# Forget gates' running sums: the triangle made on chip, and their store and first loads back issued by ScalarE

## The chip, the cores and the metric

The kernel runs on one core of a Trainium2 chip. The core has five engines, each with its own queue of instructions worked off in order: TensorE (PE; its weight loads are PEld), VectorE (DVE), ScalarE (ACT), GpSimd (POOL) and SyncE (SP), which here only issues DMAs. Engines wait for each other and for DMAs by semaphores. The metric is the device time of one execution in microseconds, lower being better; several runs are given by their median.

## The reference

A trunk of two layers over 1040 tokens (16 learned meta tokens and 1024 inputs) of width 1024. Each layer normalises, projects with one combined matrix, runs four heads of differential attention and eight heads of forgetting attention, gates both with SiLU, projects back and adds to the residual. Only the forgetting heads use the sums that the change touches:

```python
fq = ...; fk = ...; fv = ...                       # (b, 8 heads, tokens, 64)
log_f = jax.nn.log_sigmoid(ff.astype(jnp.float32) + forget_bias[l])
cum_logf = jnp.transpose(jnp.cumsum(log_f, axis=1), (0, 2, 1))   # (b, 8, tokens)
...
s = jnp.einsum('bhqd,bhkd->bhqk', qb, k) * scale   # forgetting_attention
s = s + cq[..., None] - cum_logf[:, :, None, :]
s = jnp.where(positions[None, :] <= pq[:, None], s, -jnp.inf)
p = jax.nn.softmax(s, axis=-1)
```

## The kernel before, in words

Tokens lie in nine blocks (80 tokens, seven of 128, 64), three blocks to a chunk, and the work on a layer is woven from two streams. The first is attention: 8 pairs of heads p, of which p = 0 to 3 are differential and p = 4 to 7 forgetting, each over three chunks. The second, the fills, are the projections: units k, q, v and g (gate) for each pair, in the order of the table ORDER. The order on TensorE is written out by the program (it is followed as emitted); on the other engines a scheduler sets the order, and SyncE's DMAs stand in an order of their own.

Weights come as 128x2x128 pieces by SyncE (line 254, tile wst, four buffers), are split into two parts (whi by ScalarE or GpSimd, lines 261 and 263; wlo by GpSimd or VectorE, line 265; eight buffers each), and feed TensorE's matmuls into pj (line 181, the line of every matmul).

The unit v2 (the values of the first forgetting heads) also projects the forget gates, eight columns, into ffz (z in the code). When its last block is done, log_forget computes the log-sigmoid by a chain of small VectorE operations on 128x72 (lines 544 to 561, with one exponential on ScalarE, line 546); line 561 writes the result to ffz. Some time later, by the program's model of TensorE's time, cumulate is emitted: it needs the upper triangle of ones (tile upper, which has the name tc, three buffers), multiplies each block's ffz with it (sums within a block, nine products into three sc tiles in PSUM, 4 passes in float32), and line 577 on VectorE adds the last sum of the block before while it writes the row crow (8 heads x 1040, a cb tile; two buffers). Line 579 stores crow to DRAM (cscr). When the first chunk of a forgetting pair begins, line 823 loads two rows of cscr back, each broadcast over 128 partitions, into cb tiles; line 656 on VectorE adds them to the scores of that head.

Around cumulate stand, in ScalarE's order, lines 778 and 780 (two copies of po, the attention output that TensorE has just finished, into ta), line 664 (the exponential of the last differential scores, tile e), and line 428 (q's two parts from pj). VectorE's line 716 then combines the two exponentials of a differential pair in e, which TensorE turns (tp, line 185). Line 804 makes TensorE's column sums of ta (sc<-ones,ta).

A constant of two 128x128 tables in bfloat16 (cb16: identb, the identity, and trib, 1e30 above the diagonal and 0 elsewhere) is loaded once at the start, for other uses.

Of the kernel before, what the change touches and what calls it, by code (L numbers as in the profile page):

```python
# [13 lines left out]
ALU = mybir.AluOpType  # L14

P = 128
# [4 lines left out]
T = N_META + SEQ  # L21
# [46 lines left out]
C_ID, C_U, C_DM, C_DM0 = 0, 128, 256, 256 + T  # L68
# [18 lines left out]
def trunk_kernel(ctx, tc, x, meta, norm_gain, w_in, fbias, lq1, lk1, lq2, lk2,  # L87
                 subln, w_out, fgain, cst, cstb, rope, out):
    nc = tc.nc
# [7 lines left out]
    dma = nc.sync.dma_start  # L97
# [4 lines left out]
    identb, trib = cb16[:, 0:P], cb16[:, P:2 * P]  # L102
# [25 lines left out]
    def st(tag, w, dt=F32, bufs=None):  # L128
        bufs = bufs or {"tc": TCB}.get(tag, 3)
        return sb.tile([P, w], dt, name=tag, tag=tag, bufs=bufs)  # L130

    def big(tag, bufs, dt=F32):
        return sb.tile([P, T], dt, name=tag, tag=tag, bufs=bufs)
# [25 lines left out]
    cscr = dr.tile([depth, 8, T], F32, name="cscr")  # L159
# [19 lines left out]
    def mm(o, a, b, start, stop, passes=1):  # L179
        n = b.shape[-1]  # L180
        nc.tensor.matmul(o, a, b, start=start, stop=stop)  # L181
        pe.add(b.dtype == BF16, max(n * passes * COL, 0.056))
# [29 lines left out]
    def proj_ps(tag="pj"):  # L212
        return ps.tile([P, 512], F32, name=tag, tag=tag, bufs={"pj": 2, "sc": SB, "tp": TB}[tag])
# [326 lines left out]
    def log_forget(l, z, box):  # L540

        n = NB * 8
        az = st("tc", CW)[:, :n]
        nc.vector.scalar_tensor_tensor(az, z, -1.0, z, ALU.mult, ALU.max)
        e = st("tc", CW)[:, :n]
        nc.scalar.activation(e, az, AF.Exp, scale=-1.0)

        d = st("tc", CW)[:, :n]
        nc.vector.tensor_scalar(d, e, 2.0, None, ALU.add)
        nc.vector.reciprocal(d, d)  # L550
        s = az
        nc.vector.tensor_tensor(s, e, d, ALU.mult)
        w = d
        nc.vector.tensor_tensor(w, s, s, ALU.mult)
        q = e
        nc.vector.tensor_scalar(q, w, 1.0 / 15, None, ALU.mult)
        for i in (13, 11, 9, 7, 5, 3):
            nc.vector.scalar_tensor_tensor(q, q, 1.0 / i, w, ALU.add, ALU.mult)
        nc.vector.scalar_tensor_tensor(q, q, 1.0, s, ALU.add, ALU.mult)
        nc.vector.tensor_scalar(z, z, 0.0, None, ALU.min)  # L560
        nc.vector.scalar_tensor_tensor(z, q, -2.0, z, ALU.mult, ALU.add)

        def cumulate():
            crow = big("cb", 2)
            upper = st("tc", CW)
            dma(out=upper[:, 0:P], in_=cst[:, C_U:C_U + P])
            for c in range(3):
                pt = proj_ps("sc")
                for j in range(3 * c, 3 * c + 3):
                    sz = BE[j] - BS[j]  # L570
                    o = BS[j] - CS[c]
                    mm(pt[:8, o:o + sz], z[:sz, j * 8:(j + 1) * 8], upper[:sz, :sz], True, True, 4)
                for j in range(3 * c, 3 * c + 3):
                    o = BS[j] - CS[c]
                    sz = BE[j] - BS[j]
                    prev = crow[:8, BS[j] - 1:BS[j]] if j else zero1[:8, :]
                    nc.vector.tensor_scalar(crow[:8, BS[j]:BE[j]], pt[:8, o:o + sz], prev, None,
                                            ALU.add)
            dma(out=cscr[l], in_=crow[:8, :])
            box["cum"] = True  # L580
            when["cum"] = pe.t + LCUM
        return cumulate
# [226 lines left out]
    def attention(l, box):  # L809


        units = [Unit(l, p, s, c, box) for p in range(8) for c in range(3)
                 for s in range(1 if p < 4 else 2)]

        def score(u, step):
            if not u.begun:
                u.begun = True
                if u.c == 0 and u.s == 0:
                    box["sp"] = u.p
                    for s in range(0 if u.diff else 2):  # L820
                        cb = box["cb", s] = big("cb", 2)
                        h = 2 * (u.p - 4) + s
                        dma(out=cb, in_=cscr[l, h:h + 1, :].to_broadcast([P, T]))
            u.score(*step)

        def there(u):

            return all(x in box and when.get(x, 0.0) <= pe.t + SLACK
                       for x in (("k", u.p, u.c), ("q", u.p, u.c), "cum")[:2 if u.diff else 3])

        late = []
        todo = units[0].score_steps()
        yield 0.0, ("k", 0, 0)
        yield 0.0, ("q", 0, 0)
        while todo:
            yield pe.evicted[0], None
            score(units[0], todo.pop(0))
        for i, u in enumerate(units):
            nx = units[i + 1] if i + 1 < len(units) else None
            todo = nx.score_steps() if nx else []  # L840
            free = EB - 3
            if nx and nx.diff:
                free = 2 * free - 1
            if nx and nx.p != u.p and not nx.diff:
                free = 0
            n = u.nblk
            seq = [("t", j) for j in range(TB)]
            for j in range(n):
                seq.append(("a", j))
                if j + TB < n:  # L850
                    seq.append(("t", j + TB))
            nt = due = 0
            yield u.ready, ("v", u.p, 0)
            box["vp"] = u.p
            for k, (what, j) in enumerate(seq):
                if late and pe.t >= late[0][0]:
                    late.pop(0)[1]()
                    yield 0.0, None
                if what == "t":
                    u.transp(j)  # L860
                    nt += 1
                else:
                    yield u.ev[j][2], ("v", u.p, j)
                    u.av(j)
                yield 0.0, None
                due += nt >= FR0 and k % FR1 == FR1 - 1
                if todo and (nt == n or (free > 0 and due > 0)) and there(nx):
                    free -= 1
                    due -= 1
                    yield pe.evicted[0], None  # L870
                    score(nx, todo.pop(0))
                    yield 0.0, None
            for t0, f in late:
                yield t0, None
                f()
            late = u.finish()
            while todo:
                yield 0.0, ("k", nx.p, nx.c)
                if not nx.diff:
                    yield 0.0, "cum"  # L880
                yield pe.evicted[0], ("q", nx.p, nx.c)
                score(nx, todo.pop(0))
                yield 0.0, None
        for t0, f in late:
            yield t0, None
            f()
# [327 lines left out]
```

## Time and profile before

| | us |
|---|---|
| median of 3 runs | 1623.01 |
| lowest, highest of them | 1619.45, 1624.98 |
| the profiled execution's own time | 1622.79 |
| its span (first to last instruction) | 1620.9 |

| engine | busy us | share of the span |
|---|---|---|
| PE | 1486.1 | 92% |
| PEld | 1419.7 | 88% |
| DVE | 1056.3 | 65% |
| ACT | 829.6 | 51% |
| POOL | 688.5 | 42% |

How to read the profile: it is one execution taken by the hardware profiler, in microseconds from the span's start. An operation is named by line, engine, operation and "out<-in". Where an engine stood idle ahead of an instruction, the idle time and what ended it stand in brackets ("[16.30 <-DMA tc<-in_cst_dram]"); a wait for several things is put down to the one that came last. The chain of waits follows the work back from the last instruction. A table of stretches gives each engine's busy time in a stretch and the clock granted to TensorE (1.00 is 2.4 GHz, 0.50 is 1.2 GHz).

### The profile page before, as it was taken

What the parts mean: (1) busy time and instruction counts of PE and PEld (TensorE: products, weight loads), DVE (VectorE), ACT (ScalarE), POOL (GpSimd) and SP (SyncE); (2) the same over time, 40 slices, a digit from 0 to 9 for tenths busy, and PEclk for the clock granted to TensorE, in tenths of its full rate; (3) what the DMA queues carried; (4) which work ended last, traced back from release to release, by engine and by line L of the source; (5) the groups of instructions that cost most, each with busy time, mean ns of one, the idle gap of its engine ahead of it and who ended that gap; (6) DMA issues with size and microseconds to landing.
All of it is one profiled execution on the core that took longest, in us unless ns stands there. A gap on an engine that the chain in (4) does not pass through costs nothing.

```text
span 1620.9 us, 30144 instructions
## 1 busy us (share of the span) xinstructions
PE 1486.1 (92%) x9932; PEld 1419.7 (88%) x9932; DVE 1056.3 (65%) x3024; ACT 829.6 (51%) x2067; POOL 688.5 (42%) x1125
## 2 busy tenths in 40 slices
PE   6988999978999999987998999999599999996897
PEld 5988999977999999887988898999599999995897
DVE  6588867864756565666655986596556555657554
ACT  6455556533655565543334655565256555655543
POOL 3453423312444344456756243240244442443664
PEclk9999999998999999988999999999799999998999
DMA  9342313202232323464434242131222232334554
GB/s 240 86 100 60 97 46 63 60 19 71 69 68 63 103 58 99 151 184 133 146 78 104 62 96 73 33 75 28 64 58 67 58 93 57 92 114 143 151 148 137
DMA packets 181469, 147.86 MB, mean 91 GB/s; under 512 B 19624, under 2 KB 176864, under 8 KB 181312
## 3 DMA queue, kind: packets, MB, share of 16 engines
q1 hardware_dynamic: 181312, 145.93, 33.9%
q8 instruction: 79, 1.29, 0.3%
q14 instruction: 78, 0.64, 0.1%
HBM read 117.49 MB, written 28.38 MB: 90 GB/s over the span
## 4 chain that ended last, share of the span: by engine, by line
PE 57%; DVE 11%; DMA 8%; issue 6%; POOL 3%; ACT 2%; SPq 0%; DVEq 0%; POOLq 0%; ACTq 0%
PE pj L181 36%; PE sc L181 8%; PE po L181 7%; PE tp L185 6%; DMA wst<-in_w_out_dram 3%; DMA wst<-in_w_in_dram 2%; DVE wlo L265 2%; POOL wlo L265 1%; DVE e L656 1%; DMA oscr<-ta 1%; DMA actl<-oscr 1%; DVE actl L430 1%; DVE atl L748 1%; DMA tc<-in_cst_dram 1%; DVE kt L430 1%
## 5 line engine op out<-in xcount | busy, mean ns | idle before, releaser
L181 PE MATMUL pj<-acth,whi 128*128 128x320 f32 (+2 forms) x1536 | 519.5, 338 | 15.8 <-DVE hc L942 9.9
L181 PE MATMUL pj<-acth,wlo 128*128 128x320 f32 (+2 forms) x1536 | 498.6, 325 | 0.0
L181 PE MATMUL pj<-actl,whi 128*128 128x320 f32 (+2 forms) x1536 | 498.4, 324 | 0.0
L265 POOL TENSOR_TENSOR wlo<-wst,whi 128x256 fp32r<-128x256 f32 (+1 forms) x320 | 251.6, 795 | 185.4 <-ACT whi L261 140.1
L181 PEld LDWEIGHTS pj<-acth,whi 128*128 128x128 f32 x1536 | 296.9, 193 | 19.4 <-DVE hc L942 6.6
L181 PEld LDWEIGHTS pj<-acth,wlo 128*128 128x128 f32 x1536 | 296.0, 193 | 0.5
L181 PEld LDWEIGHTS pj<-actl,whi 128*128 128x128 f32 x1536 | 294.6, 192 | 0.4 <-DVE actl L430 0.4
L664 ACT ACTIVATE e<-e,mn 80x80 f32<-80x80 f32 (+8 forms) x288 | 225.7, 784 | 123.5 <-DVE mn L656 121.0
L748 DVE TENSOR_TENSOR atl<-tp,ath 128x320 fp32r<-128x320 f32 (+8 forms) x432 | 191.6, 449 | 81.8 <-ACT ath L747 77.6
L747 ACT ACTIVATE ath<-tp 128x320 fp32r<-128x320 f32 (+8 forms) x432 | 168.3, 404 | 128.3 <-PE tp L185 119.1
L261 ACT ACTIVATE whi<-wst 128x256 fp32r<-128x256 f32 (+1 forms) x304 | 124.6, 415 | 139.7 <-PE pj L181 53.0
L181 PE MATMUL sc<-kt,qq 128*128 128x296 f32 (+9 forms) x480 | 175.6, 368 | 15.8 <-DVE mn L656 11.5
L185 PE MATMUL tp<-ident,e 128*128 128x128 f32 (+2 forms) x1080 | 179.8, 274 | 0.7 <-POOL e L697 0.3
L697 POOL TENSOR_SCALAR e<-e,rl 80x80 f32<-80x80 f32 (+2 forms) x144 | 109.0, 758 | 161.6 <-DVE rl L696 151.1
L181 PE MATMUL po<-ath,v 128*128 128x256 f32 (+5 forms) x576 | 164.9, 327 | 10.1 <-ACT ath L747 10.1
L181 PE MATMUL pj<-whi,acth 128*128 128x256 f32 (+3 forms) x576 | 166.6, 289 | 4.1 <-DVE v L430 3.3
L181 PE MATMUL pj<-wlo,acth 128*128 128x256 f32 (+3 forms) x576 | 163.6, 284 | 2.8 <-POOL wlo L265 1.4
L181 PE MATMUL pj<-whi,actl 128*128 128x256 f32 (+3 forms) x576 | 163.1, 283 | 0.8 <-POOL actl L406 0.8
L181 PE MATMUL sc<-kt,ql 128*128 128x296 f32 (+9 forms) x480 | 158.2, 332 | 0.0
L181 PE MATMUL po<-atl,v 128*128 128x256 f32 (+5 forms) x432 | 137.3, 318 | 18.2 <-DVE atl L748 17.9
L185 PEld LDWEIGHTS tp<-ident,e 128*128 128x128 f32 (+2 forms) x1080 | 136.5, 139 | 6.5 <-POOL e L697 1.9
L265 DVE TENSOR_TENSOR wlo<-wst,whi 128x256 fp32r<-128x256 f32 (+1 forms) x128 | 88.5, 696 | 62.4 <-POOL whi L263 53.0
(166 smaller groups left out, 2483.5 us busy)
## 6 DMA issues: line engine op xcount, KB each, us to landing
wst<-in_w_in_dram SPq DMA_DIRECT2D x256, 128.0 KB
wst<-in_w_out_dram SPq DMA_DIRECT2D x192, 128.0 KB
cb<-cscr SPq DMA_DIRECT2D x16, 520.0 KB
cb<-in_rope_dram SPq DMA_DIRECT2D x20, 320.0 KB
cb<-in_rope_dram SPq DMA_DIRECT2D x16, 384.0 KB
oscr<-ta SPq DMA_DIRECT2D x26, 160.0 KB
cb<-in_rope_dram SPq DMA_DIRECT2D x12, 336.0 KB
oscr<-ta SPq DMA_DIRECT2D x20, 192.0 KB
```

The source lines that it names most:

```text
L181: nc.tensor.matmul(o, a, b, start=start, stop=stop)
L185: nc.tensor.transpose(o, a, idn)
L261: nc.scalar.activation(hi, sg_, AF.Copy)
L265: eng.tensor_tensor(lo, sg_, hi.bitcast(F32), ALU.subtract)
L430: nc.vector.tensor_tensor(lo, src, hi.bitcast(F32), ALU.subtract)
L656: nc.vector.tensor_tensor_reduce(e[rows, a:b], pt[rows, :b - a], bias(a, b)[rows, :], op0=ALU.add, op1=ALU.min, scale=1.0, scalar=least, a ...
L664: nc.scalar.activation(e[rows, :ext], e[rows, :ext], AF.Exp, scale=-1.0, bias=mn[rows, len(pcs) - 1:len(pcs)], accum_out=l[rows, :])
L697: nc.gpsimd.tensor_scalar(e[rows, :ext], e[rows, :ext], r[rows, 0:1], 1.0, ALU.mult, ALU.mult)
L747: nc.scalar.activation(ah[:kz, n0:w], tp[:kz, n0:w], AF.Copy)
L748: nc.vector.tensor_tensor(al[:kz, n0:w], tp[:kz, n0:w], ah[:kz, n0:w].bitcast(F32), ALU.subtract)
```

## The change

The triangle is no longer loaded from DRAM: VectorE computes min(trib, 1) + identity into the same tile from the two bfloat16 tables. The store of crow and the two loads back for p = 4, the first forgetting pair, are issued by ScalarE; the loads back for p = 5 to 7 stay with SyncE.

```diff
@@ -563,7 +563,7 @@
         def cumulate():
             crow = big("cb", 2)
             upper = st("tc", CW)
-            dma(out=upper[:, 0:P], in_=cst[:, C_U:C_U + P])
+            nc.vector.scalar_tensor_tensor(upper[:, 0:P], trib, 1.0, identb, ALU.min, ALU.add)
...
-            dma(out=cscr[l], in_=crow[:8, :])
+            nc.scalar.dma_start(out=cscr[l], in_=crow[:8, :])
...
-                        dma(out=cb, in_=cscr[l, h:h + 1, :].to_broadcast([P, T]))
+                        load = nc.scalar.dma_start if u.p == 4 else dma
+                        load(out=cb, in_=cscr[l, h:h + 1, :].to_broadcast([P, T]))
```

The changed kernel has one line more, so line 823 is 824 there. TensorE's and GpSimd's orders are unchanged. On ScalarE, at the place of the sums in layer 0 (tc is the logarithm's tile, ta the two copies of po, e the differential scores, qq a part of q):

```order
 L261 ACTIVATE whi<-wst 128x256
 L546 ACTIVATE tc<-tc 128x72
+L579 DMA cscr<-cb 8x1040
 L778 ACTIVATE ta<-po,sgs_82 128x384
 L780 ACTIVATE ta<-po 128x384
-L664 ACTIVATE e,ls<-e,mn 128x976
+L824 DMA cb<-cscr 128x1040
+L664 ACTIVATE e,ls<-e,mn 128x976
+L824 DMA cb<-cscr 128x1040
 L428 ACTIVATE qq<-pj 64x336 x2
```

The store now stands on ScalarE ahead of the two copies, and the two loads stand around the exponential; the same holds in layer 1.

On SyncE, the same place in layer 0 (line 601 loads and line 790 stores attention outputs, line 254 loads weights):

```order
 L790 DMA oscr<-ta 128x336
 L254 DMA wst<-in_w_in_dram 128x2x128 x8
-L566 DMA tc<-in_cst_dram 128x128
-L579 DMA cscr<-cb 8x1040
-L601 DMA ta<-oscr 128x336
-L823 DMA cb<-cscr 128x1040
-L790 DMA oscr<-ta 128x384
-L823 DMA cb<-cscr 128x1040
+L601 DMA ta<-oscr 128x336
+L790 DMA oscr<-ta 128x384
 L254 DMA wst<-in_w_in_dram 128x2x128 x4
```

Four issues leave SyncE's order, and the two that stood among them close up.

On VectorE, the place in layer 1 (tc<-cb_67 is the triangle made from the tables; lines 660 and 656 evict scores):

```order
 L558 SCALAR_TENSOR_TENSOR tc<-tc 128x72 x6
 L559 SCALAR_TENSOR_TENSOR tc<-tc 128x72
+L566 SCALAR_TENSOR_TENSOR tc<-cb_67 128x128
 L561 SCALAR_TENSOR_TENSOR ffz<-tc,ffz 128x72
 L577 TENSOR_SCALAR cb<-sc,zero_79 8x80
 L577 TENSOR_SCALAR cb<-sc,cb 8x128 x7
+L577 TENSOR_SCALAR cb<-sc,cb 8x64
 L660 TENSOR_SCALAR e,mn<-sc 128x488
-L577 TENSOR_SCALAR cb<-sc,cb 8x64
 L656 ISA e,mn<-sc,dm,mn 128x488
```

The new operation stands between lines 559 and 561, and the last of the sums has moved ahead of the eviction of line 660; in layer 0 only the new operation is added, at the same place.

## Rows read from the trace of the kernel before

**Rows 1.** The page's first line: span of the profiled execution.
```profile
span 1620.9 us, 30144 instructions
```

**Rows 2.** TensorE's waits, longest first: us in total, times, longest us.
```profile
PE sc L181 <- DMA tc<-in_cst_dram: 33.8, 2, 17.5
PE po L181 <- DVE atl L748: 17.9, 17, 3.1
```

**Rows 3.** Chain that ended last, both layers: start us, us, what.
```profile
365.98 5.37 DMA tc<-in_cst_dram
...
1157.03 6.25 DMA tc<-in_cst_dram
```

**Rows 4.** Timeline, layer 0: start us, us, instruction [idle before <-releaser].
```profile
365.98 0.23 DVE L559 SCALAR_TENSOR_TENSOR tc<-tc 128x72 f32<-128x72 f32 x1
366.25 0.23 DVE L561 SCALAR_TENSOR_TENSOR ffz<-tc,ffz 128x72 f32<-128x72 f32 x1
371.48 3.43 PE L181 MATMUL sc<-tc,ffz 80*8 80x80 f32 x18 [16.30 <-DMA tc<-in_cst_dram]
```

**Rows 5.** Timeline, layer 1, the same place.
```profile
1157.30 0.23 DVE L561 SCALAR_TENSOR_TENSOR ffz<-tc,ffz 128x72 f32<-128x72 f32 x1
...
1163.41 3.41 PE L181 MATMUL sc<-tc,ffz 80*8 80x80 f32 x18 [17.53 <-DMA tc<-in_cst_dram]
```

**Rows 6.** Busy us (instructions) by stretch: length, PE, PEld, DVE, ACT, POOL, PEclk, DMA share, GB/s.
```profile
376.50:480.00 103.50, 103.50 (x709) 100.19 (x708) 59.86 (x194) 57.20 (x143) 46.31 (x86) 1.00 0.30 75
1168.40:1275.00 106.60, 106.17 (x725) 101.62 (x725) 62.30 (x199) 57.85 (x146) 47.08 (x96) 1.00 0.28 73
1158.00:1163.30 5.30, 0.00 (x0) 0.00 (x0) 0.00 (x0) 0.00 (x0) 0.00 (x0) 0.50 0.58 84
366.00:370.00 4.00, 0.00 (x0) 0.00 (x0) 0.45 (x2) 0.00 (x0) 0.00 (x0) 0.50 0.36 57
358.00:359.00 1.00, 0.00 (x0) 0.00 (x0) 0.17 (x1) 0.80 (x2) 0.51 (x1) 0.50 0.64 131
375.00:376.00 1.00, 1.00 (x7) 0.91 (x8) 0.93 (x5) 0.00 (x0) 0.00 (x0) 1.00 0.00 0
```

**Rows 7.** VectorE's groups by form, 340 to 380 us: busy us, mean ns.
```profile
L432 DVE SCALAR_TENSOR_TENSOR v<-pj,v 128x128 fp32r<-128x128 f32 x6 | 1.7, 287 | 1.5 <-ACT v L428 1.5
...
L552 DVE TENSOR_TENSOR tc<-tc 128x72 f32<-128x72 f32 x1 | 0.7, 723 | 0.0
```

**Rows 8.** Timeline: a matmul that TensorE starts on VectorE's signal.
```profile
703.70 0.48 DVE L748 TENSOR_TENSOR atl<-tp,ath 80x320 fp32r<-80x320 f32 x1
...
704.23 0.41 PE L181 MATMUL po<-atl,v 80*128 80x320 f32 x1 [1.02 <-DVE atl L748]
```

**Rows 9.** Timeline, layer 0, behind the restart: SyncE, ScalarE, VectorE, TensorE.
```profile
376.25 0.34 SPq L579 DMA_DIRECT2D cscr<-cb  x1
...
377.22 0.48 ACT L780 ACTIVATE ta<-po 128x384 f32<-128x384 f32 x1
...
377.71 1.11 ACT L664 ACTIVATE e<-e,mn 128x976 f32<-128x976 f32 x1
378.06 0.32 SPq L823 DMA_DIRECT2D cb<-cscr  x1
...
379.41 1.24 DVE L716 SCALAR_TENSOR_TENSOR e<-e,rl 128x976 f32<-128x976 f32 x1
380.43 0.45 ACT L428 ACTIVATE qq<-pj 64x336 fp32r<-64x336 f32 x1 [1.51 <-PE pj L181]
...
383.97 0.83 PE L185 MATMUL tp<-ident,e 128*80 128x128 f32 x6
```

**Rows 10.** Timeline, layer 1: the last sum on VectorE, and TensorE's tp.
```profile
1168.44 0.27 DVE L577 TENSOR_SCALAR cb<-sc,cb 8x64 f32<-8x64 f32 x1
...
1176.77 0.83 PE L185 MATMUL tp<-ident,e 128*80 128x128 f32 x6
```

**Rows 11.** VectorE's evictions that use the loaded sums: ns min/median/max, first and last start.
```profile
L656 DVE CUSTOM_DVE_ANT_0 e<-sc,cb x144: 222/521/668, 397.5 to 1481.0; 80x80 f32<-80x80 f32 x16, 128x208 f32<-128x208 f32 x16, 128x336 f32<-128x336 f32 x16, 128x464 f32<-128x464 f32 x16
```

## The prediction, made before the changed kernel was run

> **What bounds the kernel now.** I read the page first: the profiled execution has a span of 1620.9 us [rows 1], against 1622.79 us for its own time, so 1.89 us lie around the span; the median of the three runs shown, 1623.01 us, is 0.22 us above that execution. TensorE is busy for most of the span, so I next read what TensorE waits for. Its longest wait by far is the one that this change touches: two waits of 33.8 us together, put down to the load of the triangle into tile tc, while the next cause on the list has 17.9 us spread over 17 waits [rows 2]. The chain of work that ended last says the same: it runs through the triangle's load for 5.37 us in layer 0 and 6.25 us in layer 1 [rows 3].
>
> That a wait is put down to one cause does not mean that all of it goes. In layer 0 TensorE has stood for 16.30 us when it restarts at 371.48. The other operand of its first matmul, ffz, is finished by VectorE's line 561 at 366.25 + 0.23 = 366.48 [rows 4]. Up to there the wait belongs to the forget gates' own chain, which the change leaves alone; only the stretch behind it, 371.48 - 366.48 = 5.00 us, is the triangle's. In layer 1 it is 1163.41 - (1157.30 + 0.23) = 5.88 us [rows 5]. In those stretches neither ScalarE nor GpSimd does anything, and VectorE nothing but the end of the chain; so in the stretches from 366 and from 1158 no third thing becomes ready, only the transfer is awaited [rows 6]. The reader is to see a 16 to 17 us wait of which about a third is the load.
>
> **The change part by part.** (1) The triangle's load goes, and with it a DMA that could start only when the tile's buffer was free, that is, behind the logarithm's chain [rows 3, 4]. That opens 5.00 + 5.88 = 10.88 us.
>
> (2) In its place VectorE makes the triangle with one operation of 128x128 between lines 559 and 561, so on the path. No row has this form. The nearest by shape and operation is the three-operand operation of line 432 on 128x128, 287 ns [rows 7]; I take 0.29. From below, line 561 itself needs 0.23 for 72 columns [rows 4]; from above, one operation of this same chain took 723 ns [rows 7]. It runs behind line 559 on the engine that also wrote the tile before it, its source was loaded at the start, and I add 0.03 for the gap between two operations (366.25 - 366.21 [rows 4]). Cost 0.32 us a layer, bounds 0.26 and 0.75. A gain is excluded, since the operation is new on the path.
>
> (3) TensorE now starts on VectorE's signal and not on a landing. Rows of such starts: line 748 ends at 703.70 + 0.48 = 704.18 and its matmul starts at 704.23 [rows 8], 0.05 us. In the chain the start came 0.13 after the landing (365.98 + 5.37 = 371.35 to 371.48 [rows 3, 4]). I take 0.13, with 0.05 as the other bound.
>
> So layer 0 restarts at 366.48 + 0.32 + 0.13 = 366.93 in place of 371.48, a gain of 4.55 us, and layer 1 at 1157.53 + 0.32 + 0.13 = 1157.98 in place of 1163.41, a gain of 5.43. Sum 9.98 us.
>
> (4) TensorE's clock. In the idle stretch the granted clock was at 0.50, the 1.2 GHz level, already in 358 to 359, and was back at 1.00, 2.4 GHz, in 375 to 376, some 4 us after the restart [rows 6]. A wait that is 5 us shorter still contains the fall, so the slow restart stays as it is: 0.
>
> (5) The store and the first two loads back move from SyncE to ScalarE. ScalarE pays three issues a layer; SyncE's rows give 0.34 and 0.32 us for one [rows 9]. The first waits for VectorE's last sum; in layer 0 that is about 4.77 us after the restart (the store's start, 376.25 - 371.48). Behind it in ScalarE's order stand lines 778 and 780, which wait for TensorE until later still, so this wait holds nobody: 0. The second, the first load, waits for the store to land, and behind it stands line 664, the exponential of the last differential scores. The store landed 1.81 us after its issue (376.25 to 378.06 [rows 9]). Counted from the restart: store 4.77, landed 6.58, load issued with 0.35 (a little above both rows) by 6.93. Line 780 ended at 377.22 + 0.48, that is 6.22, and line 664 started at once; now it starts at 6.93, 0.71 later. From line 664's start to the end of VectorE's line 716 are 379.41 + 1.24 - 377.71 = 2.94 us, so the scores are ready at 9.87. TensorE turns them (tp) at 383.97 - 371.48 = 12.49 [rows 9]. Slack 2.62 us: cost 0. The second load is issued behind line 664; line 428, the next on ScalarE, stood idle for 1.51 us [rows 9], which covers 0.71 + 0.35. In layer 1 the tp is at 1176.77 - 1163.41 = 13.36 [rows 10], more slack still. There the last sum (0.27 us, line 577 on 8x64 [rows 10]) now stands ahead of an eviction that it followed; the slack covers this too.
>
> (6) SyncE loses four issues and three waits a layer. Behind them stand a gate's load, a store, and weight loads that wait for buffers which TensorE's own progress frees; none of them has TensorE waiting in the 103.5 us from 376.5 on, where it is busy throughout [rows 6]. Worth 0. The second load back is issued about a microsecond later after the restart than by SyncE, and what the loads bring is first used at 397.5 [rows 11], some 17 us behind that issue.
>
> What is late next: nothing for a hundred microseconds in either layer (106.17 of 106.60 us busy from 1168.4 on [rows 6]). All that follows is started by engines that follow TensorE, so I let the whole gain reach the end. Sum: 1620.9 - 9.98 + 1.89 = 1612.8, and with the median's 0.22 about 1613.0 us.
>
> **The rivals.** First, **ScalarE is held longer than SyncE's row says**. The store goes out while the last weight loads may still be in flight. With a landing time L after its issue, line 716 ends at 4.77 + L + 0.35 + 2.94 = 8.06 + L after the restart, so TensorE waits from L = 12.49 - 8.06 = 4.43 us in layer 0 and 13.36 - 8.06 = 5.30 us in layer 1. If the store fared like the triangle's load, 5.37 and 6.25 us, it would cost 0.94 + 0.95 = 1.9 us: 1614.9. For it: that load shows what a small transfer behind weight loads takes [rows 3]. Against it: the store now goes out behind those loads, not among them. The Trainium skill, "DMA: Bandwidth & Descriptors", section "Issuing engines are not separate DMA queues", speaks against the move: DMAs of all engines run on the same 16 DMA engines, and another issuer saves only sequencer time. By that rule the move can gain nothing of itself and the store can be delayed by SyncE's loads, which is this rival; no row of this trace has a DMA issued by ScalarE.
>
> The **slower side** is the same mechanism taken further: it decides at (L - 4.43) + (L - 5.30) = 9.98, L = 9.9 us. At 12.5 us it would cost 15.3 and give 1613.0 + 15.3 = 1628.3. Nothing in the rows lands so late for so few bytes, but ScalarE's issuing is unseen.
>
> Third, **the gain is given back later**: one layer's gain is taken up by a later wait that does not follow TensorE, such as the output projection's weight loads. That leaves 4.55 to 5.43 us of gain, 1617.6 to 1618.5, say 1618.0. Against it speaks the stretch without waits behind each restart.
>
> Fourth, **the change does not do what it says**: another operand, listed behind the triangle because it came a little sooner, ends the wait at nearly the old time. Then 1623.0. Against it are the idle engines in the two stretches.
>
> **How the numbers follow.** Forecast with holds up to 1.9 us: 0.78. Given back in part: 0.10. No effect: 0.07. Slower through the hold: 0.05. The time is the forecast's, 1613.0. Its parts' bounds move it by 0.9 up (0.75 for the operation in both layers) and by 0.3 down; the three runs of before lie from 3.6 below to 2.0 above their median. So the range begins at 1609.5; above it takes in the case of one layer's gain and ends at 1618.0. It leaves out no effect, slower, and half of the third case. A change of 0.3% is 4.9 us, about what a measurement of this kernel can tell from none: faster means below 1618.1. Faster: 0.78 and half of the third case, 0.83; same: the other half and no effect, 0.12; slower 0.05.
>
> **What would show it.** Right: the two waits of TensorE at its sums' matmuls become 11 to 13 us each, released by VectorE's line 561; ScalarE's line 664 starts about 7 us after the restart; no wait of TensorE at tp some 12 us after it; SyncE's weight loads keep their distance to TensorE. Wrong: a wait for DMA still at the sums, a wait of TensorE for line 716, a store's landing above 4.4 us, or later waits, in the output projection above all, that grow by what was gained.

## The result and the profile after

The changed kernel took 1615.8 us (median of 8 runs, 1611.18 to 1617.7) where the kernel before, run beside it, took 1622.35 (8 runs, 1619.45 to 1627.74). The ratio is 0.9949, with a 95% interval of 0.9933 to 0.9965. On the 1623.01 us from which the prediction started that is 1614.7 us, 8.3 us less (5.7 to 10.9 by the interval), against 10.0 forecast. The profiled execution took 1612.99 us, of which 1611.2 are its span; the span of before is 1620.9 [rows 1].

The page's first line, its two queues of DMAs that SyncE and ScalarE issue (packets, MB, share of 16 engines), and TensorE's longest waits (us in total, times, longest us), all of the changed kernel:

```profile
span 1611.2 us, 30139 instructions
...
q1 hardware_dynamic: 180416, 143.60, 33.7%
q10 hardware_dynamic: 608, 2.20, 0.5%
...
PE sc L181 <- DVE ffz L561: 23.1, 2, 11.7
PE po L181 <- DVE atl L748: 18.9, 18, 3.1
```

The wait for the triangle's load, 33.8 us [rows 2], is now one of 23.1 us for VectorE's line 561, the end of the forget gates' own chain. It is still the longest that TensorE has: the change cuts a stop short and does not fill it. Queue q10 is new; it carries ScalarE's DMAs.

The timeline at the place, VectorE and TensorE, layer 0 and then layer 1, in the changed kernel (start us, us, instruction, [idle before <-releaser]):

```profile
369.11 0.23 DVE L559 SCALAR_TENSOR_TENSOR tc<-tc 128x72 f32<-128x72 f32 x1
369.26 0.28 DVE L566 SCALAR_TENSOR_TENSOR tc<-cb 128x128 f32<-128x128 bf16 x1
369.46 0.23 DVE L561 SCALAR_TENSOR_TENSOR ffz<-tc,ffz 128x72 f32<-128x72 f32 x1
369.75 3.73 PE L181 MATMUL sc<-tc,ffz 80*8 80x80 f32 x18 [11.34 <-DVE ffz L561]
...
1153.69 0.23 DVE L561 SCALAR_TENSOR_TENSOR ffz<-tc,ffz 128x72 f32<-128x72 f32 x1
1153.97 3.73 PE L181 MATMUL sc<-tc,ffz 80*8 80x80 f32 x18 [11.74 <-DVE ffz L561]
```

Read against [rows 4, 5]: the products now start 0.06 us (369.75 - 369.69) and 0.05 us behind line 561, where it was 5.00 and 5.88. The stops themselves are 4.96 and 5.79 us shorter (16.30 to 11.34, 17.53 to 11.74), 10.75 us together, which is a little more than the 9.98 forecast. The median fell by about 2 us less. The interval is too wide to tell 8.3 from 10.75, but if something gave back a part, the place to look first is right behind the restart. Four stretches there, two of before and then two of after (columns as in [rows 6]; of interest are PE's busy time and number of matmuls, and PEclk, the granted clock):

```profile
371.60:374.20 2.60, 2.60 (x14) 1.70 (x13) 1.08 (x4) 0.00 (x0) 0.00 (x0) 0.50 0.00 0
1163.50:1166.20 2.70, 2.70 (x15) 1.78 (x15) 1.15 (x4) 0.00 (x0) 0.00 (x0) 0.50 0.00 0
```

```profile
369.80:374.60 4.80, 4.80 (x22) 3.20 (x23) 2.89 (x10) 0.00 (x0) 0.00 (x0) 0.50 0.39 82
1154.00:1159.60 5.60, 5.60 (x24) 3.88 (x25) 3.04 (x10) 0.00 (x0) 0.00 (x0) 0.50 0.55 75
```

In both kernels TensorE restarts at 0.50, the 1.2 GHz level. Before, that lasted at least 2.6 and 2.7 us of work; after, at least 4.8 and 5.6. How much it costs can be read at the next fixed point, the turning of the scores (tp), which stood 12.49 and 13.36 us behind the restart [rows 4, 5, 9, 10]. After:

```profile
383.14 0.83 PE L185 MATMUL tp<-ident,e 128*80 128x128 f32 x6
1168.63 0.61 PE L185 MATMUL tp<-ident,e 128*80 128x128 f32 x4
```

These are 13.39 and 14.66 us behind it, 0.90 and 1.30 us more. All of that is spent by the end of the last matmul into po (called the pairs' end below): from the first product to there the stretch grew from 5.22 and 5.21 us to 6.12 and 6.50. Net, then, in these two executions the place gives 10.75 - 2.20 = 8.55 us. That is close to the ratio's 8.3, but the forecast's 9.98 lies in the ratio's interval too, and the spans of the two executions differ by 9.7. Stretches away from the place differ by as much as the 2.20 us: up to the first stop the execution of the changed kernel is 3.2 us longer, from layer 0's tp to the second stop 2.8 us shorter, and behind layer 1's tp 1.6 us shorter. The times alone don't show the loss; the trace of one execution does.

ScalarE's side of the change, layer 0 (ACT are its activations, ACTq the DMAs that it issues):

```profile
374.57 0.54 ACTq L579 DMA_DIRECT2D cscr<-cb  x1
375.90 0.58 ACT L778 ACTIVATE ta<-po,sgs 128x384 f32<-128x384 f32 x1 [10.66 <-PE po L181]
376.38 0.48 ACT L780 ACTIVATE ta<-po 128x384 f32<-128x384 f32 x1
376.41 0.37 ACTq L824 DMA_DIRECT2D cb<-cscr  x1
376.83 1.11 ACT L664 ACTIVATE e<-e,mn 128x976 f32<-128x976 f32 x1
376.88 0.38 ACTq L824 DMA_DIRECT2D cb<-cscr  x1
```

The store had landed 376.41 - 374.57 = 1.84 us after its issue, when the load that waits for it was issued (1.81 from SyncE [rows 9]). The load's issue falls inside line 780's time, and line 664 starts 0.45 us after line 780, where it was 0.49 [rows 9]. ScalarE is not held here.

### The profile page after: what moved, and what is told of

It reads as the page before. It is cut to its first block, busy times and chain, and to the rows that moved or that the text cites. A ratio compares the mean times of both kernels' runs of the same rounds, so it can differ in the third digit from the quotient of the medians.

```text
span 1611.2 us, 30139 instructions
## 1 busy us (share of the span) xinstructions
PE 1487.1 (92%) x9932; PEld 1419.7 (88%) x9932; DVE 1056.2 (66%) x3026; ACT 826.8 (51%) x2067; POOL 690.0 (43%) x1125
## 4 chain that ended last, share of the span: by engine, by line
PE 58%; DVE 10%; DMA 7%; issue 6%; POOL 4%; ACT 2%; SPq 0%; DVEq 0%; POOLq 0%; ACTq 0%
PE pj L181 37%; PE sc L181 8%; PE po L181 7%; PE tp L185 6%; DMA wst<-in_w_out_dram 2%; DMA wst<-in_w_in_dram 2%; POOL wlo L265 2%; DVE wlo L265 1%; DVE e L656 1%; DMA actl<-oscr 1%; DVE atl L748 1%; DVE kt L430 1%; DMA oscr<-ta 1%; DVE tc L423 1%; DVE tc L422 1%
```

## The experiments

My theory after the result: the whole gain is the triangle's; the move to ScalarE is worth nothing; and the missing 2 us are the slow restart. The rivals: the move contributes or costs, or the gain is given back far behind the place. Each run has its ratio to the kernel before, run on the same chip.

**The triangle alone.** Made by VectorE as in the change, all DMAs left on SyncE:

```diff
-            dma(out=upper[:, 0:P], in_=cst[:, C_U:C_U + P])
+            nc.vector.scalar_tensor_tensor(upper[:, 0:P], trib, 1.0, identb, ALU.min, ALU.add)
```

> The kernel before with the triangle made on VectorE and nothing else; store and loads back stay with SyncE. Theory A (the whole gain is the triangle's load taken off TensorE's wait): the same as the full change, ratio to before 0.995 (0.993 to 0.997), TensorE's two waits at the sums together 23 us against 33.8. Theory B (part of the gain comes from taking DMAs out of SyncE's order): only part of it, ratio 0.997 to 0.999.

Measured: 1611.58 us, ratio 0.9935 (0.9915 to 0.9955). TensorE's wait is that of the changed kernel, and so is the slower restart (5.99 and 6.13 us from the first product to the pairs' end):

```profile
PE sc L181 <- DVE ffz L561: 23.0, 2, 11.9
```

**The move alone.** The triangle still loaded, the store and the first two loads back on ScalarE:

```diff
-            dma(out=cscr[l], in_=crow[:8, :])
+            nc.scalar.dma_start(out=cscr[l], in_=crow[:8, :])
...
-                        dma(out=cb, in_=cscr[l, h:h + 1, :].to_broadcast([P, T]))
+                        load = nc.scalar.dma_start if u.p == 4 else dma
+                        load(out=cb, in_=cscr[l, h:h + 1, :].to_broadcast([P, T]))
```

> The kernel before with store and first loads back issued by ScalarE and nothing else; the triangle is still loaded by SyncE. Theory A: no change, ratio 1.000 within 0.002, TensorE's two waits at the sums still 33 to 34 us and put down to the load. Theory B: a gain of its own, ratio 0.996 to 0.998. Theory C (ScalarE is held by the store's landing and that costs): above 1.001, with a wait of TensorE at tp some 12 us after the restart.

Measured: 1621.78 us, ratio 1.0001 (0.9988 to 1.0014), with the load still waited for:

```profile
PE sc L181 <- DMA tc<-in_cst_dram: 34.2, 2, 17.6
```

In layer 0 of this kernel ScalarE is held as the prediction had it: the load's issue waits for the store to land, and line 664 behind it starts 0.68 us late (0.71 forecast). It costs nothing that can be measured:

```profile
379.98 0.36 ACTq L824 DMA_DIRECT2D cb<-cscr  x1
380.38 1.11 ACT L664 ACTIVATE e<-e,mn 128x976 f32<-128x976 f32 x1 [0.68 <-DMA cscr<-cb]
```

The two parts are apart: the triangle is the whole change, the move is nothing to within 0.14%. This is as the Trainium skill has it ("DMA: Bandwidth & Descriptors", section "Issuing engines are not separate DMA queues"): whichever engine issues, the transfer runs on the same 16 DMA engines.

**The restart at full clock.** The changed kernel with filler ahead of the products, matmuls whose results are overwritten:

```diff
+                for _ in range(95 if c == 0 else 0):
+                    nc.tensor.matmul(pt[:, 0:256], identb, cb16, start=True, stop=True)
```

> The changed kernel with 95 extra matmuls of 256 columns (identity times a table, results overwritten) put ahead of the first sums' product, where TensorE stands idle, so that its clock need not fall. Theory K (the half clock after the restart costs what the changed kernel lost against the forecast): granted clock 1.00 at the restart, from the first product to the end of po 3.5 to 4.0 us in place of 6.12 and 6.50, and 4 to 6 us less than the changed kernel, ratio to before 0.991 to 0.992. Rival (the stretch behind the restart is long for another reason, an eviction or an operand): still above 5.5 us per layer and no gain over the changed kernel, ratio 0.995.

The granted clock stays at 1.00 through the stop and the restart (first row: up to the products; second: from them on). The last row is the end of the pairs in layer 0; the products began at 369.34:

```profile
355.00:369.00 14.00, 13.41 (x117) 11.90 (x115) 8.48 (x29) 4.36 (x13) 7.34 (x10) 1.00 0.30 60
369.40:374.00 4.60, 3.83 (x28) 2.79 (x29) 2.98 (x11) 0.00 (x0) 0.00 (x0) 1.00 0.51 81
...
373.92 0.28 PE L181 MATMUL po<-atl,v 128*128 128x256 f32 x1
```

From products to pairs' end it is 374.20 - 369.34 = 4.86 us, and 4.88 in layer 1, instead of 6.12 and 6.50. So the slow stretch is the clock's: against this kernel it costs 1.3 and 1.6 us in the changed kernel and cost only 0.35 in the kernel before. The 3.5 to 4.0 us that I had expected are not reached, because at full clock TensorE waits 0.77 us for an eviction of VectorE inside the stretch. The time did not follow, against what I had expected: 1616.34 us, ratio 0.9966 (0.9954 to 0.9978), not better than the changed kernel's. In that kernel the instructions behind the products also stand in a somewhat different order, and waits elsewhere are longer (for GpSimd's gs 9.2 us against 6.1); which of these took the gain back was not settled.

**Does the restart depend on how long the stop is?** The changed kernel with eight and then sixteen operations more behind the triangle:

```diff
+            for _ in range(8):
+                nc.vector.tensor_scalar(upper[:, 0:P], upper[:, 0:P], 1.0, None, ALU.mult)
```

> The changed kernel with eight operations more of 128x128 on VectorE behind the triangle, which leave its values as they are: each stop of TensorE is longer by some 1.3 to 1.9 us, 12.6 to 13.6 us. Measured is the stretch from the first product to the last copy of the pairs (po end), 5.2 us in the kernel before behind stops of 16 to 17 us and 6.1 and 6.5 us in the changed one behind stops of 11.3 and 11.7. Theory 'a shorter stop leaves a longer slow restart': 5.6 to 6.1 us in both layers. Rival 'the slow restart scatters by itself': values outside 5.5 to 6.3 us or over 0.6 us apart.

> The changed kernel with sixteen operations more of 128x128 on VectorE behind the triangle, which leave its values as they are: e6_delay8's eight lengthened TensorE's stops to 13.3 and 13.6 us, so here 15.2 to 15.7 us. Behind 13.3 and 13.6 us the stretch from the first product to the last copy of the pairs took 5.31 and 5.95 us. Theory 'a shorter stop leaves a longer slow restart': 5.1 to 5.6 us in both layers, as behind the 16 to 17 us of the kernel before (5.22 and 5.21). Rival 'it scatters by itself': at least one value of 5.9 us or more.

The products of both kernels, eight operations first:

```profile
373.67 3.52 PE L181 MATMUL sc<-tc,ffz 80*8 80x80 f32 x18 [13.30 <-DVE tc L568]
1160.59 3.73 PE L181 MATMUL sc<-tc,ffz 80*8 80x80 f32 x18 [13.57 <-DVE tc L568]
```

```profile
370.81 3.44 PE L181 MATMUL sc<-tc,ffz 80*8 80x80 f32 x18 [15.33 <-DVE tc L568]
1160.52 3.73 PE L181 MATMUL sc<-tc,ffz 80*8 80x80 f32 x18 [15.78 <-DVE tc L568]
```

With all stops beside each other (us, one execution of each kernel; the stretch is from the first product to the pairs' end):

| kernel | stop, layers 0 and 1 | stretch |
|---|---|---|
| after | 11.34, 11.74 | 6.12, 6.50 |
| triangle alone | 11.16, 11.89 | 5.99, 6.13 |
| eight operations | 13.30, 13.57 | 5.31, 5.95 |
| sixteen operations | 15.33, 15.78 | 5.22, 6.15 |
| before | 16.30, 17.53 | 5.22, 5.21 |
| move alone | 16.62, 17.59 | 5.18, 5.60 |

By the rule written down ahead, the rival holds: sixteen operations gave 6.15 us in layer 1, and eight gave values 0.64 apart. The stretch scatters between 5.2 and 6.5 us and is no plain function of the stop, though all four behind the stops under 12 us are near its upper end. What sets it in one execution stays open.

**Filling the stop instead of shortening it.** What remained was 23.1 us of waiting for VectorE's chain. The planner (fills) gives out the products at the first chance after the due time in box["lft"]. That time had been set at the end of the value unit before, so it was long past when the gates were ready, and the products went right behind the last block of values. One line sets it anew (on the changed kernel):

```diff
                 box["lf"] = log_forget(l, z, box)
+                box["lft"] = pe.t + 14.0
```

> The changed kernel with one line more: when the last block of v2 hands over the logarithm's chain, the due time of the sums is set to 14 us (of the program's model of TensorE's time) behind it, so that the products no longer follow that block at once. Theory D (the 23 us of waits that are left come from the order alone, since TensorE has q4's projection to do): the two waits vanish or fall below 3 us each, the clock does not fall, 18 to 28 us less than the changed kernel, ratio to before 0.977 to 0.984. Rival E (the chain on ScalarE and VectorE is stretched by their other work, and ScalarE, now busy, is held at the store and at the first load back): waits of the same size show up at tp or at q's operands, gain over the changed kernel below 8 us, ratio 0.990 or above.

Measured: 1603.88 us, ratio 0.9885 (0.9867 to 0.9904). The waits fall from 23.1 to 7.9 us:

```profile
PE sc L181 <- DVE ffz L562: 7.9, 2, 4.6
```

This lies between the two forecasts: some 10 us less than the changed kernel (0.9885 against 0.9949), neither theory D's 18 to 28 nor rival E's under 8, and the two waits of 3.25 and 4.62 us are not below 3 each. One clause of theory D failed outright: the clock still falls behind these shorter stops. In layer 1 it stands at the low level for 9 us of work without a break, longer than in the changed kernel:

```profile
1149.10:1158.20 9.10, 9.10 (x41) 7.50 (x42) 4.63 (x15) 1.29 (x3) 0.73 (x2) 0.50 0.24 56
```

So a stop of 4.62 us did not bring a shorter slow stretch than one of 11.74, though with other work behind it. Two kernels below with this order show the same place at the low level for some 9 us too (9.1 in the repetition, 8.7 without the move).

> The changed kernel with the products due 20 and not 14 planned us behind the last block of values. Theory 'the rest of the wait is only lead': the 7.9 us that e4_defer left at the sums fall to 0 to 2, no wait takes their place, time 1596 to 1600 us, ratio 0.984 to 0.986. Rival 'the lead is used up': VectorE's chain is stretched by the further work that is placed beside it, or the differential scores come too late and TensorE waits at tp or at the output instead; time 1602 us or more, ratio 0.987 or above.

Measured: 1605.54 us, ratio 0.9888 (0.9871 to 0.9906), again 7.9 us of waits. The kernel turned out to be the last one, instruction for instruction: at the end of the unit fills sets the due time once more, 8 planned us ahead, so 14 and 20 both become 8. As an experiment on the lead it says nothing; as a repetition it agrees with the last one to 0.0003, well within the intervals.

Is the change worth the same under that cover? First the products deferred in the kernel before, with the load, and then with the triangle but without the move:

> The kernel before, triangle still loaded, all DMAs on SyncE, with the forget gates' products due later by one line (as in e4_defer, where that line on the changed kernel gave 1603.9 us and left 7.9 us of waits on VectorE's chain). Theory 'the two gains add': the load can still start only when the chain has freed the tile's buffer, so behind the longer chain it is waited for again, 5 to 6 us a layer; the waits at the sums are 18 to 20 us, put down to the load, and the time is some 8 to 11 us above e4_defer's, 1612 to 1615 us, ratio 0.993 to 0.996. Rival 'any cover would have done': the later products hide the load as well, the waits are 8 to 10 us and the time is e4_defer's, 1602 to 1606 us, ratio 0.987 to 0.990.

> The kernel before with the triangle made by VectorE and the products due later, the store and the loads back left on SyncE: e4_defer without the move to ScalarE. There the store and the loads stand among ScalarE's other work and not in an idle stretch. Theory 'the issuer is worth nothing here either': ratio to before within 0.002 of e4_defer's 0.9885, 1602 to 1606 us. Rival 'the move holds ScalarE or frees SyncE once there is other work': over 3 us from e4_defer, below 1601 (ScalarE was held) or above 1607 us (SyncE was the hindrance).

With the load: 1612.81 us, ratio 0.9938 (0.9924 to 0.9951), the waits at the sums 4.75 and 9.89 us:

```profile
374.12 3.72 PE L181 MATMUL sc<-tc,ffz 80*8 80x80 f32 x18 [4.75 <-DVE ql L432]
1160.89 3.60 PE L181 MATMUL sc<-tc,ffz 80*8 80x80 f32 x18 [9.89 <-DMA tc<-in_cst_dram]
```

In layer 1 the load is waited for again, until 5.3 us behind the chain's end, but not only because the chain has to free its buffer. SyncE issued it 3.1 us behind the chain's end, right after line 602, which had waited 7.7 us for a store of attention outputs:

```profile
1158.28 0.34 SPq L602 DMA_DIRECT2D ta<-oscr  x1
1158.66 0.43 SPq L567 DMA_DIRECT2D tc<-in_cst_dram  x1
```

The products then started 1160.89 - 1158.66 = 2.23 us after the issue, where it had been 5.50 and 6.38 in the kernel before (371.48 - 365.98, 1163.41 - 1157.03 [rows 3, 4, 5]). In layer 0 the products start 1.6 us behind the chain's end, and the profile names an eviction and not the load; so the waits are 14.6 us together and not the 18 to 20 expected, while the time is as expected. With the triangle on VectorE and no move: 1607.43 us, ratio 0.9901 (0.9884 to 0.9918), within 0.002 of 0.9885. The time is 0.4 us beyond the rival's bound of 1607, but the kernel before was 3.3 us slower on this chip (1624.23 against 1620.91), so the ratio decides; the kernel with the move took 1605.54 us on the same chip. These runs show no effect of the issuer here either, and the triangle is still worth some 6 to 9 us (0.9938 against 0.9885 to 0.9901).

**More cover.** The due time behind the values made really longer, 16 and 22 planned us, with that line left in; the second also with the triangle loaded and everything on SyncE, that is, on the kernel before:

```diff
             if u[0] in "vh":
-                box["lft"] = pe.t + LLF
+                box["lft"] = pe.t + (22.0 if u[0] == "v" else LLF)
```

> The changed kernel with the products due 16 planned us behind the values and the planner's own 8 us no longer in force behind the values (e8_defer20 turned out to be e4_defer instruction for instruction, since those 8 us, set at the unit's end, replaced its 20). More projection work now stands ahead of the products. Theory 'the rest of the wait is only lead': the 7.9 us at the sums fall to 0 to 2 and the clock does not fall there; time 1593 to 1599 us, ratio 0.981 to 0.985. Rival 'the lead is used up': VectorE's chain grows with the evictions placed beside it, or TensorE waits elsewhere instead, at tp or at the pairs; 1602 us or more, ratio 0.987 or above.

> As e9_due16, with 22 planned us. If 16 are enough to cover the chain, this is the same, within 0.002 of e9_due16's ratio; if the wait only needs more lead, it is lower, down to 0.980; if the forget gates' scores are now late for their use, TensorE waits at tp or the pairs and it is above e9_due16 by 0.002 or more.

> The kernel before, triangle loaded and all DMAs on SyncE, with the products due 22 planned us behind the values, as in e9_due22. Theory 'the triangle's load is worth its wait alone': with that much work ahead of the products the load is hidden, the waits at the sums are 0 to 2 us and the ratio is e9_due22's within 0.002; so the change would be worth nothing in a kernel whose order leaves room. Rival 'the load costs in other ways too': above e9_due22 by 0.003 or more, through waits of 5 us or more at the sums or elsewhere.

Measured: 16 us, 1602.23 us, ratio 0.9863 (0.9842 to 0.9884); 22 us, 1591.84 us, 0.9814 (0.9791 to 0.9837); 22 us with the load, 1593.16 us, 0.9817 (0.9796 to 0.9839). With 16 us the waits at the sums vanish and the clock does not fall, as the theory had it, but the ratio lies between its 0.985 and the rival's 0.987. With 22 us the ratio is lower, though no wait at the sums was left to remove. With 22 us and the load, the load goes out and the products follow without any wait, in layer 1 too:

```profile
379.65 0.42 SPq L567 DMA_DIRECT2D tc<-in_cst_dram  x1
...
382.88 2.04 PE L181 MATMUL sc<-tc,ffz 80*8 80x80 f32 x18
```

Once TensorE has other work at this place, the triangle's load is hidden and the whole change is worth nothing that these runs can tell: 0.9814 with it, 0.9817 without, each to within 0.0023. One more look at the stretch from 355 to 375 us in the kernel before, in the changed one and in the changed one with 22 us shows what filling does (columns as in [rows 6]):

```profile
355.00:375.00 20.00, 3.70 (x21) 2.24 (x20) 7.71 (x28) 3.05 (x8) 4.80 (x8) 0.57 0.27 56
```

```profile
355.00:375.00 20.00, 8.66 (x49) 6.66 (x49) 11.95 (x41) 4.73 (x16) 7.33 (x10) 0.66 0.28 61
```

```profile
355.00:375.00 20.00, 18.76 (x126) 17.65 (x125) 13.73 (x47) 10.32 (x26) 10.01 (x16) 1.00 0.31 71
```

TensorE is busy for 18.76 of the 20 us and the clock does not fall, so the slow restart goes as well. Between 16 and 22 us one thing stays open: neither waits at the products, yet the first is 12.5 us longer in its span (1602.6 against 1590.1). Some 7 us of that stand in the waits of the pairs for their turned scores (for line 749 21.5 against 15.8 us, for line 748 5.4 against 3.8); why they are longer was not worked out.

## Why the prediction was right, point by point

The time, 1613.0 us, was within the measurement's interval, and the mechanism was the forecast one. The interval (a gain of 5.7 to 10.9 us) can't tell the forecast's 10.0 from the 8.3 measured, so what follows on sizes rests on the traces. By its steps:

- **Steps 1 to 3, the load's wait goes: right, slightly undersized.** 10.75 us of waiting went instead of 9.98. The triangle's operation was priced at 0.32 us a layer; it takes 0.28 us by its row, but it starts before line 559's row has ended, and line 561 comes only 0.35 us after line 559's start, where it was 0.27 [rows 4]. On the path it costs 0.08 us. TensorE started 0.05 us behind VectorE, the lower of the two bounds.
- **Step 4, "the slow restart stays as it is: 0": the mis-sized term.** In the profiled execution it cost 0.90 + 1.30 = 2.20 us. That the shorter stop would still contain the fall of the clock was right, but from it did not follow that the slow stretch behind it stays as long. One row [rows 6] told where the clock was high again, and only roughly: the prediction read some 4 us behind the restart, and the stretch from 374.0 to 374.5, with a clock of 0.62, puts it at some 2.9. No row told how far the return depends on when the work begins. That the shorter stop is the reason is not shown: the stretch took 6.15 us behind a stop of 15.78 too, and the triangle alone, with a slow restart like the changed kernel's, gave 0.9935, the whole forecast gain (0.9938). That the slow restart left the total near the forecast is in part luck. An honest bound would have been the stretch at full clock on one side and all of it at the low one on the other.
- **Step 5, the move: right.** In the kernel with the move alone line 664 was held by the store's landing for 0.68 us in layer 0, against 0.71 forecast, and the slack covered it (1.0001). In the changed kernel the hold did not occur: the slow restart had delayed the two copies ahead of line 664 by 0.9 us and the store by 0.05, so the store had landed in time. The sign "line 664 starts about 7 us after the restart" came true there (376.83 - 369.75 = 7.08) by luck, through the late copies and not through the store.
- **Step 6 and what is late next: right.** No new wait took the gain; the stretches away from the two places scatter by 1.6 to 3.2 us, in both directions, without a sign of it.
- **The rivals.** None came. The store landed in 1.84 us, far from the 4.43 us from which it would have cost anything, and the move alone gave 1.0001. "The gain is given back later" is closest in size, but what the trace shows as given back was given back within 6.5 us of the restart, and not by a transfer.

What the prediction did not ask is what the remaining stop is worth. It read the stop up to line 561 as belonging to the chain, "which the change leaves alone". That was right for the forecast; but that stop was the larger part, and with it covered the change itself has no effect that these runs can tell.

## What to carry to other kernels

When an engine waits for two things, measure the stretch between the two arrivals: that stretch alone is what removing the later one gives, and here it could be read to within 0.8 us. Then ask why the engine has nothing else to do there: an order that covers the wait (here two lines in the planner, 1.4% with 16 planned us and 1.9% with 22, of which a part is not explained) can be worth several times the removal of its last part (0.5%) and makes that removal needless. Covering two thirds of it (23.1 to 7.9 us) did not keep the clock up. Moving a DMA's issue to another engine is worth trying only where the profile shows an engine late because of its own issuing; here the move gave nothing (1.0001).

## What the runs showed of the hardware

- The time that TensorE works at the low clock behind a stop is not a constant of this kernel: with the same instructions behind it, the stretch took 5.2 to 6.5 us, against 4.9 at full clock (0.77 of it a wait). Behind a stop of only 4.62 us the granted clock stood at 0.50 for 9.1 us in which TensorE was busy throughout.
- ScalarE's DMA issues (0.37 to 0.54 us by their rows) did not delay its activations: line 780 began 0.48 us after line 778 and line 664 0.45 us after line 780 with an issue in between. What held an activation, in the kernel with the move alone, was the wait of such an issue for an earlier store to land (0.68 us).
- The same 64 KB load was used 5.50 and 6.38 us after its issue where eight weight loads of 128 KB had been issued in the 12 us before, and 2.23 us after it where the last weight load lay 9 us back and one other load, of 192 KB, had been issued just ahead (the kernel before with the products deferred, layer 1).
- Small operations on VectorE overlap by their rows: one of 128x128 that takes 0.28 us by its row put off its successor by 0.08 us.
